# Paged softmax of a decoder layer: the maximum over the partitions moved from GpSimd to TensorE and VectorE

## Chip, cores and metric

One core of a Trainium2 chip runs the whole layer. The metric is the device time of one execution in microseconds (us). The engines are named as the profile does: PE is TensorE's matmul and PEld its weight load, DVE is VectorE, ACT is ScalarE, POOL is GpSimd, SP is SyncE, which here issues DMAs. A trailing q (POOLq, SPq) is an engine's sequencer.

## What is computed

One step of a decoder layer for two kinds of input at once: a prompt of 1024 tokens (plus 16 meta tokens) and eight sequences that each decode one token against 4096 cached keys and values in pages of 128. Every token goes through a projection, differential attention (4 heads, two softmax maps each) beside a causal convolution, an output projection and a SwiGLU FFN. The change touches the decoding sequences' attention alone:

```python
def sample_layer(x, ck, cv, conv_state, page_table, lw, li):
    ...
    k_past = ck[page_table].reshape(Bd, past, N_DIFF_HEADS, 2, HEAD_DIM).astype(k.dtype)
    v_past = cv[page_table].reshape(Bd, past, N_DIFF_HEADS, V_HEAD_DIM).astype(v.dtype)
    ...
    o = diff_attend(q, k_all, v_all, q_pos, k_pos, lam, alibi_slopes())

def diff_attend(q, k, v, q_pos, k_pos, lam, slopes):
    s = jnp.einsum('bqhjd,bkhjd->bhjqk', q, k) * (HEAD_DIM ** -0.5)
    s = s - slopes[None, :, None, None, None] * dist
    ...
    p = jax.nn.softmax(s, axis=-1)
    a = p[:, :, 0] - lam * p[:, :, 1]
    return jnp.einsum('bhqk,bkhe->bqhe', a.astype(v.dtype), v)
```

## The kernel before

The prompt is worked in stages that overlap: projections and convolution, attention by head `h` and block `i` of 128 queries (`attn`), output projection by blocks (`c_one`), then the FFN in steps of 128 hidden columns (`ffn`). Its f32 matmuls are three fp32r matmuls of a high and a low part (`mm3`, L149 to L151); ACT casts the high part of each weight tile and DVE or POOL subtracts to get the low one (L138 and L140 before the FFN, L957 and L959 in it).

The paged attention of the eight sequences is cut into units that are sprinkled over the prompt's work. A unit of keys (`dec_scores`) loads two pages of 128 keys through SP's queue, multiplies each with the query by one POOL instruction (L681), and one DVE instruction sums the products to scores (L691); keys lie on the partitions, so `s` is 128 partitions by 33 pages by 8 maps (the 33rd page is the token itself). Sixteen units are one sequence. Then `dec_max` adds the bias (L699), puts in the token's own score (L704), takes the maximum over the pages on DVE (L706, giving 128x8), and takes it over the partitions with POOL's `partition_all_reduce` (L708). `dec_exp` subtracts it on DVE (L713) and takes the exponential on ACT (L714). A unit of values (`dec_values`) loads two pages of values; in groups of two units PE multiplies them with the probabilities as weights (L733), four pages side by side in four column groups of the array.

`dec_units` sets the order of units: 23 units of keys first (16 and a lag of 7); then, as soon as the tokens' own keys exist (`"k" in nat`), maximum and exponential of the first sequence at once, and after that two units of values and two of keys in turn. A later sequence's exponential is written two units of keys (`elag`) after its maximum. `dec_step` takes units at given rates: about one a block of attention, one a block of `c_one`, 2.45 at each `fill` of the FFN. When the units are used up, the eight tokens' own output projection and FFN (`sample_units`) follow in the same way. All is emitted with a priority 400 instructions ahead, and the framework's planner, which simulates a timeline, sets the final order on each engine; every engine then works its instructions in that order. SP's queue carries page loads, weight loads and most others, in order; a load whose buffer is not free holds up those behind it.

Other names used later: in `attn`, POOL's power L565 (`or`) normalises four blocks of a head, ACT's L567 applies it, PE's L572 transposes the result; DVE's L510 evaluates a score tile that PE's L508 and L509 wrote. `natural` (L607) transposes 128x8 tiles to 8x128 on PE, `row_T` (L1102) transposes 8x128 pieces. PSUM tiles from `pb` come from a ring of three.

Of the kernel before, what the change touches and what calls it, by code (L numbers as in the profile page):

```python
# [12 lines left out]
ALU = mybir.AluOpType  # L13
AX = mybir.AxisListType
SP = mybir.EngineType.SP

P = 128
# [3 lines left out]
DB = 8  # L21
# [25 lines left out]
def tile_layer(ctx: ExitStack, tc: tile.TileContext, I, O, cfg):  # L47
    nc = tc.nc
    V, S, G, T, D = nc.vector, nc.scalar, nc.gpsimd, nc.tensor, nc.sync
# [5 lines left out]
    at = ctx.enter_context(tc.tile_pool(name="at", bufs=cfg["at"]))  # L55
# [33 lines left out]
    def pdec(name):  # L89
        return ps.tile([P, 512], F32, tag="d", name=name, bufs=cfg["nd"])  # L90

    def smt(name, w, n=2, dt=F32):
        return sm.tile([P, w], dt, tag="".join(x for x in name if not x.isdigit()), name=name, bufs=n)
# [5 lines left out]
    ident = cst.tile([P, P], F32, name="ident")  # L99
# [387 lines left out]
    def attn(h, i):  # L487
# [95 lines left out]
    nat = {}  # L583
# [6 lines left out]
    ones = cst.tile([P, DB], F32, name="ones")  # L590
# [4 lines left out]
        out=own, in_=own, pattern=[[-1, DB], [0, 8]], compare_op=ALU.is_equal, fill=0.0, base=0, channel_multiplier=1  # L595
# [60 lines left out]
    def page_pair(src, b, pg, name):  # L656
        t = kv(name)[:, :1024].rearrange("p (i n) -> p i n", i=2)
        for i in range(2):
            n = b * NPG + pg + i
            lds, (v,) = nc.values_load_multi_w_load_instructions(  # L660
                pts[0:1, n : n + 1], engines=[SP], min_val=0, max_val=n_pool - 1
            )
            if len(page_dmas) >= 8:
                for ld in lds:
                    tc.add_manual_dep(ld.ins if hasattr(ld, "ins") else ld, page_dmas[-8], behind, reason="few registers at once")
            x = D.dma_start(t[:, i, :], src[bass.DynSlice(v, 1)].rearrange("o p f -> (o p) f"))  # L666
            if cfg["anchor"] and i == 0:
                tc.add_manual_dep(x.ins if hasattr(x, "ins") else x, point["now"], behind, reason="paced by the prompt's work")
            page_dmas.append(x.ins.name if hasattr(x, "ins") else x.name)
        return t  # L670

    def dec_scores(b, st):
        qB = dec.tile([P, 512], F32, tag="qB", name=f"qB{b}")
        D.dma_start(qB, qsD[b].partition_broadcast(P))
        s = dec.tile([P, NPG + 1, 8], F32, tag="s", name=f"s{b}", bufs=3)
        st[b] = s
        for pg in range(0, NPG, 2):
            kt = page_pair(ck, b, pg, f"k{b}_{pg}")
            n = b * NPG // 2 + pg // 2
            for i in range(2):  # L680
                x = G.tensor_tensor(kt[:, i, :], kt[:, i, :], qB, op=ALU.mult)  # L681
            products.append((s[:, pg : pg + 2, :], kt))
            if len(products) > cfg["rlag"]:
                head_sums(x)
            yield b

    products = []

    def head_sums(after):
        s, kt = products.pop(0)  # L690
        x = V.tensor_reduce(  # L691
            s.rearrange("p a c -> p (a c)"), kt.rearrange("p a (c d) -> p (a c) d", d=HD), axis=AX.X, op=ALU.add
        )
        if after is not None:
            tc.add_manual_dep(x.ins, after.ins.name, behind, reason="sums behind a later product")

    def dec_max(b, st):
        s = st[b]
        V.tensor_tensor(  # L699
            s[:, :NPG, :].rearrange("p g (h j) -> p (g h) j", j=2),  # L700
            s[:, :NPG, :].rearrange("p g (h j) -> p (g h) j", j=2),
            dbias.rearrange("p g h -> p (g h)").unsqueeze(2).to_broadcast([P, NPG * NH, 2]), op=ALU.add,
        )
        V.tensor_copy(s[:, NPG, :], selfs[:, b, :])  # L704
        m = smt(f"dm{b}", 8, 2)
        V.tensor_reduce(m, s.rearrange("p g c -> p c g"), axis=AX.X, op=ALU.max)  # L706
        mg = smt(f"dg{b}", 8, 2)
        G.partition_all_reduce(mg, m, P, bass.bass_isa.ReduceOp.max)  # L708
        st[b] = s, mg

    def dec_exp(b, st):
        s, mg = st[b]
        V.tensor_tensor(s, s, mg.unsqueeze(1).to_broadcast([P, NPG + 1, 8]), op=ALU.subtract)  # L713
        S.activation(s, s, AF.Exp)  # L714
        st[b] = s

    def dec_total(b, s):
        V.tensor_reduce(dsum[:, b, :], s.rearrange("p g c -> p c g"), axis=AX.X, op=ALU.add)
        V.tensor_tensor(selfa, selfa, s[:DB, NPG, :], op=ALU.add)

    def dec_values(b, st):
        a = st.pop(b)
        pv = pdec(f"pv{b}")
        vs = []
        for pg in range(0, NPG, 2):
            if not vs:
                size = min(cfg["vgrp"] if kv_n[1] else 2, (NPG - pg) // 2)
            vs.append((pg, page_pair(cv, b, pg, f"v{b}_{pg}")))
            if len(vs) == size:
                for q, vt in vs:  # L730
                    for i in range(2):
                        g = (q + i) % 4
                        x = T.matmul(  # L733
                            pv[32 * g : 32 * g + 8, :], lhsT=a[:, q + i, :], rhs=vt[:, i, :],
                            start=q + i < 4, stop=q + i >= NPG - 4, tile_position=(0, 32 * g),
                        )
                        if vt is not vs[-1][1]:
                            tc.add_manual_dep(x.ins, page_dmas[-1], together, reason="pages side by side")
                vs = []
            if pg == NPG // 2:  # L740
                dec_total(b, a)
            yield 0 if vs else size
        pvs = dec.tile([P, 512], F32, tag="gs", name=f"pvs{b}", bufs=2)
        for g in range(4):
            S.copy(pvs[32 * g : 32 * g + 8, :], pv[32 * g : 32 * g + 8, :])
            S.dma_start(pvD[b, g], pvs[32 * g : 32 * g + 8, :])

    def dec_units():
        st = {}
        ks = (b for bb in range(DB) for b in dec_scores(bb, st))  # L750
        nk, ready, exped, at = 0, 0, 0, []
        per = NPG // 2

        def softmaxes(all_=False):
            nonlocal ready, exped
            while "k" in nat and ready < (nk - len(products)) // per:
                dec_max(ready, st)
                at.append(nk)
                ready += 1
            while exped < ready and (all_ or nk >= at[exped] + cfg["elag"]):  # L760
                dec_exp(exped, st)
                exped += 1

        def keys(n):
            nonlocal nk
            for _ in range(n):
                if nk < DB * per:
                    next(ks)
                    nk += 1
                    if nk == DB * per:  # L770
                        while products:
                            head_sums(None)
                    softmaxes(nk == DB * per)
                    yield

        yield from keys(per + cfg["lag"])
        while "k" not in nat:
            yield "wait"
        softmaxes(True)
        for b in range(DB):  # L780
            for n in dec_values(b, st):
                yield
                yield from keys(n)

    dgen = dec_units()
    dst = {"done": False}

# [601 lines left out]
    sqv=1, ksp=0, asp=1, sps=1,  # L1389
    od=1, kt=0, ho=0,  # L1390
    wd='d',
    lag=7, rlag=1, elag=2,
    xn_g=(), wi_first=1, wi_e=(13, 17), sq=0,
    behind=-400, w0=7, w1=7, wi_n=1, anchor=1, wi_v=(8, 9, 10, 11, 12), taps=11, conv=400, r2_g=1, hb=5,
    vgrp=2, fing=5, ml_g=0, fend=22, cst=0, db=3, cn=6, scn=12, wo0=27, wor=2, c0=7,
    at=8, slabs=35, kv=4, p=6, dve_mul=0, rate_b=(1, 1.25, 1, 0.75), rate_c=1, rate_d=2.45, rate_s=2.2,
# [42 lines left out]
```

## Time and profile before

| | before |
|---|---|
| median of 3 runs | 1437.51 us (1437.06 to 1437.9) |
| the profiled execution | 1439.89 us |
| span of its trace | 1437.8 us |
| mean granted clock of PE | 0.976 of full speed |
| busy: PE, DVE, POOL, ACT | 1350.5, 861.1, 592.1, 548.6 us |
| HBM traffic | 183 GB/s over the span |

The trace is of one execution; its span is what the engines worked, and the execution's time holds a few microseconds around it. Busy times of different engines overlap. Matmuls are pipelined, so the end of one is modelled, and the spacing of starts says more than a duration. An idle time in brackets stands before the instruction, with what was read as its releaser; "issue" means that nothing in the profile was waited for.

### The profile page before, as it was taken

How to read it: one execution, taken by the hardware profiler on the slowest of the kernel's cores; microseconds unless marked ns; L12 is line 12 of the kernel's file. 1: busy time of each engine (PE TensorE's matmuls, PEld its weight loads, DVE VectorE, ACT ScalarE, POOL GpSimd, SP SyncE). 2: the span in 40 equal slices, each digit the busy share in tenths (PEclk: the TensorE clock that was granted, in tenths of full speed). 3: DMA queues.
4: the chain of work that ended last, by engine and by line, in shares of the span. 5: the costliest groups of instructions: out<-in, count | busy, mean ns of one | idle time of the engine just before them, and what ended most of it. 6: DMA issues, size and time to landing. Idle time of an engine off the chain costs nothing.

```text
span 1437.8 us, 21538 instructions
## 1 busy us (share of the span) xinstructions
PE 1350.5 (94%) x6960; PEld 1058.9 (74%) x6960; DVE 861.1 (60%) x1403; ACT 548.6 (38%) x1110; POOL 592.1 (41%) x479
## 2 busy tenths in 40 slices
PE   5999899988848999999999989999999999999997
PEld 4999799978847787777776767777676666567666
DVE  5689995854674567455846546474744176363157
ACT  6566878797855345212222121212121112211122
POOL 4498875544454123544636536464650000000023
PEclk9999899999979999999999999999999999999999
DMA  8210113416335538678776767787677736663554
GB/s 248 84 59 17 44 45 116 135 63 210 111 121 180 182 126 265 233 229 272 251 254 220 241 217 241 243 260 255 229 243 246 254 114 201 239 217 128 176 205 177
DMA packets 199678, 264.35 MB, mean 184 GB/s; under 512 B 16423, under 2 KB 99816, under 8 KB 199557
## 3 DMA queue, kind: packets, MB, share of 16 engines
q1 hardware_dynamic: 188912, 254.40, 53.8%
q10 hardware_dynamic: 10653, 8.57, 1.8%
q8 instruction: 55, 0.90, 0.3%
q14 instruction: 58, 0.48, 0.1%
HBM read 245.92 MB, written 17.48 MB: 183 GB/s over the span
## 4 chain that ended last, share of the span: by engine, by line
PE 48%; SPq 5%; DMA 5%; issue 4%; DVE 4%; POOL 3%; ACT 1%; POOLq 0%; DVEq 0%; ACTq 0%
PE pu L149 4%; PE pu L151 4%; PE pu L150 4%; PE pg L150 4%; PE pg L149 4%; PE dn L149 4%; PE pg L151 4%; PE dn L150 4%; PE dn L151 4%; PE pv L733 3%; DMA k<-in_cache_k 3%; SPq L666 3%; SPq L660 2%; PE mo L151 2%; PE mo L149 2%
## 5 line engine op out<-in xcount | busy, mean ns | idle before, releaser
L681 POOL TENSOR_TENSOR k<-k,qB 128x512 f32<-128x512 f32 x256 | 353.3, 1407 | 230.5 <-DMA k<-in_cache_k 159.7
L691 DVE TENSOR_REDUCE s<-k 128x16 f32<-128x1024 f32 x128 | 155.2, 1213 | 99.1 <-POOL k L681 99.0
L957 ACT CAST wH<-wr 128x1024 fp32r<-128x1024 f32 x66 | 69.1, 1048 | 239.2 <-DVE wL L959 137.3
L149 PE MATMUL dn<-wH,aH 128*128 128x512 f32 x352 | 141.9, 406 | 4.0 <-DVE y L1000 2.3
L150 PE MATMUL dn<-wL,aH 128*128 128x512 f32 x352 | 141.4, 402 | 0.0
L151 PE MATMUL dn<-wH,aL 128*128 128x512 f32 x352 | 141.3, 402 | 0.0
L149 PE MATMUL pu<-hH,wH 128*128 128x512 f32 x352 | 140.1, 398 | 0.5 <-DVE y L1000 0.5
L151 PE MATMUL pu<-hH,wL 128*128 128x512 f32 x352 | 138.7, 395 | 1.5 <-DVE wL L959 1.5
L149 PE MATMUL pg<-hH,wH 128*128 128x512 f32 x352 | 139.8, 397 | 0.0
L150 PE MATMUL pu<-hL,wH 128*128 128x512 f32 x352 | 139.5, 396 | 0.0
L150 PE MATMUL pg<-hL,wH 128*128 128x512 f32 x352 | 139.4, 396 | 0.0
L151 PE MATMUL pg<-hH,wL 128*128 128x512 f32 x352 | 139.1, 395 | 0.0
L959 DVE TENSOR_TENSOR wL<-wr,wH 128x1024 fp32r<-128x1024 f32 x66 | 92.4, 1399 | 46.6 <-ACT wH L957 19.8
L1000 DVE TENSOR_TENSOR y<-dn,y 128x512 f32<-128x512 f32 x144 | 95.8, 684 | 38.8 <-PE dn L151 38.2
L415 POOL TENSOR_TENSOR cb<-cb 128x512 f32<-128x512 f32 x80 | 103.0, 1319 | 18.3 <-ACT cb L412 9.8
L424 DVE SCALAR_TENSOR_TENSOR acc<-u,cw,acc 128x512 f32<-128x512 f32 x144 | 98.5, 747 | 0.2
L1072 POOL TENSOR_TENSOR y<-y,wfpost 128x512 f32<-128x512 f32 x10 | 14.2, 1424 | 202.0 <-ACT ft L1070 202.0
L149 PEld LDWEIGHTS dn<-wH,aH 128*128 128x128 f32 x352 | 67.8, 193 | 29.2 <-issue 6.9
L983 ACT CAST aH<-sg 128x512 fp32r<-128x512 f32 x44 | 27.2, 619 | 161.8 <-DVE sg L976 161.7
L150 PEld LDWEIGHTS dn<-wL,aH 128*128 128x128 f32 x352 | 67.4, 192 | 25.9 <-issue 10.0
L149 PEld LDWEIGHTS pu<-hH,wH 128*128 128x128 f32 x352 | 66.1, 188 | 25.9 <-issue 9.9
L149 PEld LDWEIGHTS pg<-hH,wH 128*128 128x128 f32 x352 | 66.1, 188 | 24.3 <-issue 8.6
(581 smaller groups left out, 2923.5 us busy)
## 6 DMA issues: line engine op xcount, KB each, us to landing
k<-in_cache_k SPq DMA_DIRECT2D x256, 256.0 KB
v<-in_cache_v SPq DMA_DIRECT2D x256, 256.0 KB
wr<-in_w_gate SPq DMA_DIRECT2D x22, 512.0 KB
wr<-in_w_up SPq DMA_DIRECT2D x22, 512.0 KB
wr<-in_w_down SPq DMA_DIRECT2D x22, 512.0 KB
sd<-in_w_down SPq DMA_DIRECT2D x22, 512.0 KB
sw_gate<-in_w_gate SPq DMA_DIRECT2D x20, 512.0 KB
sw_up<-in_w_up SPq DMA_DIRECT2D x20, 512.0 KB
```

What stands on the lines that cost most here:

```text
L149: T.matmul(out, lhsT=wH, rhs=xH, start=first, stop=False)
L150: T.matmul(out, lhsT=wH, rhs=xL, start=False, stop=False)
L151: mark(T.matmul(out, lhsT=wL, rhs=xH, start=False, stop=last))
L415: G.tensor_tensor(accp, accp, t, op=ALU.add)
L424: V.scalar_tensor_tensor(dst, src, cw[:, ct, k : k + 1], acc, op0=ALU.mult, op1=ALU.add)
L666: x = D.dma_start(t[:, i, :], src[bass.DynSlice(v, 1)].rearrange("o p f -> (o p) f"))
L681: x = G.tensor_tensor(kt[:, i, :], kt[:, i, :], qB, op=ALU.mult)
L691: x = V.tensor_reduce(s.rearrange("p a c -> p (a c)"), kt.rearrange("p a (c d) -> p (a c) d", d=HD), axis=AX.X, op=ALU.add)
L733: x = T.matmul(pv[32 * g : 32 * g + 8, :], lhsT=a[:, q + i, :], rhs=vt[:, i, :], start=q + i < 4, stop=q + i >= NPG - 4, tile_position=(0, ...
L957: S.copy(H[:, :1024], raw[:, :1024])
L959: V.tensor_tensor(L[:, :1024], raw[:, :1024], H[:, :1024].bitcast(F32), op=ALU.subtract)
L1000: V.tensor_tensor(y[b][:, ws], o, y[b][:, ws], op=ALU.add)
```

## The change

The maximum over the partitions becomes four small steps. `dec_rows` transposes the 128x8 maxima on PE to 8x128 in PSUM, reduces each row on DVE to 8x1, and multiplies the 8x8 identity with it on DVE, which gives a diagonal of the eight maxima. `dec_spread` multiplies a matrix of ones (8x128) with that diagonal on PE, so that all 128 partitions get the eight maxima, and copies them out of PSUM on DVE. `dec_exp` is as before. These three are written as steps in `dec_units`: `advance` is called at every unit, of keys or of values, starts at most one maximum, and moves each softmax that is under way by one step when `sgap` = 2 units have passed. Before the values of a sequence start, units of keys are written until its exponential is there, or, if keys may not run further ahead, empty units; this puts the first sequence's values some seven units of keys later.

```diff
--- before.py
+++ after.py
@@ -704,8 +704,24 @@
         V.tensor_copy(s[:, NPG, :], selfs[:, b, :])
         m = smt(f"dm{b}", 8, 2)
         V.tensor_reduce(m, s.rearrange("p g c -> p c g"), axis=AX.X, op=ALU.max)
+        st[b] = s, m
+
+    def dec_rows(b, st):
+        s, m = st[b]
+        pt = pb(f"mT{b}")
+        T.transpose(out=pt[:8, :P], in_=m, identity=ident)
+        g = smt(f"mr{b}", 1, 2)
+        V.tensor_reduce(g[:8], pt[:8, :P], axis=AX.X, op=ALU.max)
+        d = smt(f"md{b}", 8, 2)
+        V.tensor_scalar(d[:8], ident[:8, :8], g[:8], None, op0=ALU.mult)
+        st[b] = s, d
+
+    def dec_spread(b, st):
+        s, d = st[b]
+        pt = pb(f"mB{b}")
+        T.matmul(pt[:, :8], lhsT=ones[:8, 0:1].to_broadcast([8, P]), rhs=d[:8], start=True, stop=True)
         mg = smt(f"dg{b}", 8, 2)
-        G.partition_all_reduce(mg, m, P, bass.bass_isa.ReduceOp.max)
+        V.tensor_copy(mg, pt[:, :8])
         st[b] = s, mg
 
     def dec_exp(b, st):
@@ -748,18 +764,24 @@
     def dec_units():
         st = {}
         ks = (b for bb in range(DB) for b in dec_scores(bb, st))
-        nk, ready, exped, at = 0, 0, 0, []
+        nk, ready, exped, units, under = 0, 0, 0, 0, []
         per = NPG // 2
-
-        def softmaxes(all_=False):
-            nonlocal ready, exped
-            while "k" in nat and ready < (nk - len(products)) // per:
+        steps = (dec_rows, dec_spread, dec_exp)
+
+        def advance():
+            nonlocal ready, exped, units
+            units += 1
+            for x in list(under):
+                if units >= x[2] + cfg["sgap"]:
+                    steps[x[1]](x[0], st)
+                    x[1:] = x[1] + 1, units
+                    if x[1] == len(steps):
+                        under.remove(x)
+                        exped += 1
+            if "k" in nat and ready < (nk - len(products)) // per:
                 dec_max(ready, st)
-                at.append(nk)
+                under.append([ready, 0, units])
                 ready += 1
-            while exped < ready and (all_ or nk >= at[exped] + cfg["elag"]):
-                dec_exp(exped, st)
-                exped += 1
 
         def keys(n):
             nonlocal nk
@@ -770,15 +792,21 @@
                     if nk == DB * per:
                         while products:
                             head_sums(None)
-                    softmaxes(nk == DB * per)
+                    advance()
                     yield
 
         yield from keys(per + cfg["lag"])
         while "k" not in nat:
             yield "wait"
-        softmaxes(True)
         for b in range(DB):
+            while exped <= b:
+                if nk < min(DB * per, per * (b + 2) - 1):
+                    yield from keys(1)
+                else:
+                    advance()
+                    yield
             for n in dec_values(b, st):
+                advance()
                 yield
                 yield from keys(n)
 
@@ -1389,7 +1417,7 @@
     sqv=1, ksp=0, asp=1, sps=1,
     od=1, kt=0, ho=0,
     wd='d',
-    lag=7, rlag=1, elag=2,
+    lag=7, rlag=1, sgap=2,
     xn_g=(), wi_first=1, wi_e=(13, 17), sq=0,
     behind=-400, w0=7, w1=7, wi_n=1, anchor=1, wi_v=(8, 9, 10, 11, 12), taps=11, conv=400, r2_g=1, hb=5,
     vgrp=2, fing=5, ml_g=0, fend=22, cst=0, db=3, cn=6, scn=12, wo0=27, wor=2, c0=7,
```

## Rows read from the trace of the kernel before

**Rows 1.** The page, part 1: busy time of each engine, share of the span, instructions.

```profile
PE 1350.5 (94%) x6960; PEld 1058.9 (74%) x6960; DVE 861.1 (60%) x1403; ACT 548.6 (38%) x1110; POOL 592.1 (41%) x479
```

**Rows 2.** Five stages: width, busy PE, PEld, DVE, ACT, POOL, PEclk, DMA, GB/s.

```profile
427.00:437.00 10.00, 9.27 (x45) 8.74 (x45) 6.72 (x21) 8.90 (x19) 5.84 (x4) 0.55 0.07 28
...
456.00:740.00 284.00, 283.18 (x1321) 212.69 (x1320) 171.27 (x233) 85.77 (x171) 121.80 (x99) 1.00 0.69 225
740.00:775.00 35.00, 31.94 (x137) 22.40 (x137) 16.72 (x19) 9.99 (x14) 16.92 (x13) 0.90 0.62 203
...
828.00:862.00 34.00, 29.57 (x131) 20.72 (x130) 16.23 (x19) 8.34 (x12) 13.13 (x10) 0.95 0.63 217
...
1090.00:1145.00 55.00, 55.00 (x268) 35.46 (x267) 13.34 (x19) 6.97 (x12) 0.00 (x0) 1.00 0.73 241
```

**Rows 3.** Instructions of L708 and L140: count, ns min/median/max, first and last start.

```profile
L708 POOLq MODIFY_POOL_CONFIG  x16: 8/11/25, 401.6 to 1076.3; - x16
...
L140 POOLq MODIFY_POOL_CONFIG  x2: 108/108/108, 410.1 to 410.1; - x2
```

**Rows 4.** Groups by line: busy, mean ns, idle time before and its releasers.

```profile
L708 POOL PARTITION_ALL_REDUCE dg<-dm x8 | 3.1, 393 | 57.9 <-issue 35.9 <-DMA k<-in_cache_k 22.0
...
L713 DVE TENSOR_TENSOR s<-s,dg 128x264 f32<-128x264 f32 x8 | 3.5, 434 | 46.3 <-POOL dg L708 46.3
```

**Rows 5.** POOL's timeline: start, us, instruction, [idle before <-releaser].

```profile
409.71 0.39 POOL L708 PARTITION_ALL_REDUCE dg<-dm  x1 [8.11 <-issue]
417.32 2.33 POOL L140 TENSOR_TENSOR wo2L<-wo2r,wo2H 128x1024 fp32r<-128x1024 f32 x1 [7.21 <-DMA wo7r<-in_w_out]
...
424.87 1.37 POOL L565 TENSOR_TENSOR or<-ssq,mhalf 128x4 f32<-128x4 f32 x1
...
672.99 17.97 POOL L681 TENSOR_TENSOR k<-k,qB 128x512 f32<-128x512 f32 x12 [8.59 <-DMA k<-in_cache_k]
...
744.84 0.39 POOL L708 PARTITION_ALL_REDUCE dg<-dm  x1 [5.93 <-issue]
752.96 11.52 POOL L681 TENSOR_TENSOR k<-k,qB 128x512 f32<-128x512 f32 x8 [7.72 <-PE pu L151]
```

**Rows 6.** PE's timeline, five of its waits between 400 and 1145 us.

```profile
412.23 0.69 PE L508 MATMUL S<-R,L 128*128 128x392 f32 x1 [5.41 <-DVE nm L510]
...
426.73 0.47 PE L572 MATMUL oT<-ident,oh 128*128 128x128 f32 x1 [9.24 <-ACT oh L567]
...
768.19 1.90 PE L733 MATMUL pv<-v,s 128*8 128x512 f32 x8 [3.06 <-DMA v<-in_cache_v]
...
855.57 1.63 PE L733 MATMUL pv<-v,s 128*8 128x512 f32 x8 [3.95 <-DMA v<-in_cache_v]
...
1017.31 0.50 PE L149 MATMUL dn<-wH,aH 128*128 128x512 f32 x1 [1.68 <-DVE y L1000]
```

**Rows 7.** ACT's cast of wo2, from the timeline.

```profile
401.99 1.04 ACT L138 CAST wo2H<-wo2r 128x1024 fp32r<-128x1024 f32 x1
```

**Rows 8.** The chain of waits, 740 to 775 us: start, us, what.

```profile
752.96 2.54 POOL k L681 x2
755.53 1.23 DVE s L691
...
763.38 4.67 DMA v<-in_cache_v
```

**Rows 9.** The chain of waits, 826 to 862 us.

```profile
834.77 7.08 issue
```

**Rows 10.** Small PE operations in the timeline and the chain, and a weight load's gap.

```profile
386.73 0.60 PE L607 MATMUL nk<-ident,smp 128*8 128x128 f32 x4 [0.57 <-ACT kst L308]
...
1206.37 0.59 PE shT L1102 x8
...
569.24 0.19 PEld L150 LDWEIGHTS pg<-hL,wH 128*128 128x128 f32 x1 [0.86 <-issue]
```

**Rows 11.** Who waited for whom: us in total, times, the longest.

```profile
POOL k L681 <- DMA k<-in_cache_k: 159.7, 48, 9.5
```

## Prediction

> **What bounds the kernel now.** I read the page first, then one-line tables by stage, then the POOL queue, then every wait of TensorE (PE). The page says that PE is busy 1350.5 of 1437.8 us [rows 1], so only about 87 us can be won without taking work off PE, and any wait of another engine that PE doesn't feel is worth nothing. By stage, PE is full in the prompt's FFN: 283.18 us busy of 284 from 456 to 740, and 55.00 of 55 from 1090 to 1145, where pages of values still arrive but no keys are multiplied any more [rows 2]. The holes lie before 456 us (end of the prompt's attention) and in two places near 768 and 855 us, and each comes with a stretch in which the granted clock fell: mean 0.55 from 427 to 437, 0.90 from 740 to 775, 0.95 from 828 to 862 [rows 2]. The two levels are 1.2 and 2.4 GHz, so a mean of 0.90 is a fifth of the stretch at 1.2 GHz, and a stretch of width w with mean c has lost w x (1 - c) of full-speed PE time wherever PE was busy.
>
> Next the line that is changed. Ahead of each of the eight all-reduces stand two MODIFY_POOL_CONFIG, and two stand again at the next ordinary POOL instruction (for the first softmax at L140, at 410.1 us) [rows 3]. The all-reduce itself is 0.393 us, but POOL idles 57.9 us before the eight, 7.2 each, and VectorE (DVE) waits 46.3 us for them [rows 4]. The POOL queue shows the other half: 8.11 us before the all-reduce at 409.71 and 7.21 us before the next instruction, 5.93 and then 7.72 us at 744.84, and 8.59 us, the longest, behind the one at 664 [rows 5]. The releasers named for the gaps behind vary (a DMA, PE); their length hardly does, so I read them as one thing, the change of configuration back. So one softmax takes about 15 us out of POOL for 0.4 us of work, and about 6 us out of DVE, whose next instruction is the subtraction that waits.
>
> **What of this reaches PE.** Listing PE's waits shows where it counts: 5.41 us at 412.23 (DVE behind the first all-reduce), 9.24 us at 426.73, 3.06 us at 768.19, 3.95 us at 855.57, 1.68 us at 1017.31 [rows 6]. In the other softmaxes (580, 664, 921, 1083 us) PE runs on through DVE's stall, because its weights are split ahead.
>
> **Part by part.**
>
> *A, the first softmax (removed).* The wait at 426.73 is for ACT's L567, which needs POOL's `or` at 424.87, which stands in POOL's queue behind wo2L at 417.32 [rows 5]. POOL's hole in front of wo2L is 8.11 + 0.39 + 7.21 = 15.7 us. Without it wo2L would start when its cast is done: POOL was free at about 401.6, the cast ends at 401.99 + 1.04 = 403.03 [rows 7], so 417.32 - 403.1 = 14.2 us earlier, and `or` and PE's L572 with it. The 5.41 us at 412.23 lie inside these 14.2 and are not added. Against it: the new order puts up to seven units of keys in front of the first values (below), and a unit costs POOL two products; one more unit in front of `or` is 2 x 1.29 = 2.6 us by the chain's 2.54 [rows 8]. I take 14.2 - 2.6 = 11.6. The ends: 14.2 + 10 x (1 - 0.55) = 18.7, if the clock stays at 2.4 GHz in 427 to 437, which I don't count since ACT is busy 8.90 us of those 10 [rows 2]; and 6, with three such units.
>
> *B, the stalls at 768 and 855 (removed).* The chain of waits in 740 to 775 runs POOL products at 752.96 (right after the reload), DVE's sums at 755.53, the page loads that SP had held back for the buffers of those sums, value pages on their way from 763.38 for 4.67 us, PE [rows 8]. The chain to the wait at 855.57 begins with 7.08 us of "issue" on POOL at 834.77, just behind an all-reduce, and then runs the same way [rows 9]. Worth 3.06 + 35 x (1 - 0.90) + 3.95 + 34 x (1 - 0.95) = 3.06 + 3.5 + 3.95 + 1.7 = 12.2 us. Ends: 0, if value pages are late anyway; 13.9 with the 1.68 us at 1017.31, 15 us after an all-reduce.
>
> *C, work added on PE.* Per softmax a transpose of 128x8 and a spread of 8 rows to 128 partitions, which I count as two instructions since an f32 matmul of pages (L733) is two in this trace (512 for 256 pages). Nearest rows: four transposes of the same form in 0.60 us, eight 8x8 ones in 0.59 us [rows 10], so 0.15 + 2 x 0.074 = 0.30 us. Leaving the FFN's stream costs something too; behind a group of page matmuls the weight load shows a gap of 0.86 us, part of which the group itself covers [rows 10]. Ends: 8 x 0.30 = 2.4 and 8 x (0.30 + 0.86) = 9.3. I take 0.5 each, 4 us, nearer to the rows of the operations.
>
> *D, waits added on PE.* The transpose waits for DVE's L706, the spread for DVE's product with the identity; behind either stands the FFN's stream, for which everybody waits. Both come two units after what they need, and the exponential two more. PE waits on DVE in the FFN are rare, the longest before 1145 us is 1.68 [rows 6]. Ends: 0 and 16 x 1.68 = 27 us. I take 0.25 each, 4 us, because at the stage where 14 of the 16 lie PE runs without one for hundreds of microseconds [rows 2].
>
> *E, order.* Values of the first sequence start some seven units later, all else keeps its place, and the number of units is the same. One group of page matmuls that filled PE's idle time before 456 us now runs in the full stream: 1 us (0 to 1.2). The end then has some seven more units of values alone, and such a stretch runs with PE full [rows 2]: nothing. DVE gets three small instructions a softmax; by the 0.434 us of the subtraction as their upper bound [rows 4] 24 x 0.434 = 10.4 us against 46.3 us of waiting removed, on an engine busy 60% [rows 1]: nothing. Two more PSUM tiles from the ring of three are held for one DVE instruction each: nothing in the FFN, where that ring is idle; in the attention it would show as one more wait of the sort in D.
>
> Sum: -11.6 - 12.2 + 4 + 4 + 1 = -14.8 us. The profiled execution took 1439.89 us, its span is 1437.8, the median of the runs 1437.51; the difference comes from the span and is taken off the median: 1422.7 us. After A and B, what is late next is PE itself.
>
> *A rule that speaks against it.* The rows above say that a 0.393 us reduction costs POOL about 15 us. The Trainium skill, GPSIMD Engine Reference, section 4.1 (Engine selection), names GPSIMD as the engine for a reduction along the partitions and VectorE as the one not to use. By the instruction's own row that would be right; by the holes around it the trace disagrees. By that rule the sum would lose A and B and keep C, D and E.
>
> **The rivals.**
> - *More comes back* (0.12): both upper ends, 18.7 + 13.9, with C at 2.4 and no new waits: 1437.5 - 30.2 = 1407.3. For it: the clock's share is real time; against: ACT is nearly full behind A.
> - *Value pages are late anyway* (0.12): A stays, B is 0: 1437.5 - 11.6 + 9 = 1434.9. POOL waits 159.7 us for key pages in 48 places [rows 11], which no all-reduce explains; but the holes in PE come just behind the reloads.
> - *PE waits for DVE* (0.11, slower): in the added steps PE, which now is independent of the softmax, is held by DVE, which in turn sits behind sums whose products are late. At 1.68 us a step: -11.6 - 12.2 + 4 + 27 + 1 = +8.2, 1445.7, and more if the clock falls to 1.2 GHz behind it. It decides from (14.8 + 4)/16 = 1.2 us a step. For it: DVE's sums follow POOL's products, and those wait up to 9.5 us for pages [rows 11]. Against: two units lie between, and the longest DVE stalls were the ones behind the reloads.
> - *The reloads stay* (0.03, slower): another POOL instruction needs the other configuration, so the change keeps the holes and adds C, D and E: 1437.5 + 9 = 1446.5. Against: the pairs stand at L708 and at what follows it, nowhere else.
>
> **How the numbers follow.** The forecast, 1422.7, gets 0.62; its own range is 1410 to 1432. The range for 8 in 10 reaches down past the first rival and up past the second: 1405 to 1441; it leaves out the two slower rivals (0.14) and a tail. About 0.2%, 2.9 us, is what a measurement can tell from no change, so faster means under 1434.6. Faster: 0.59 of the forecast, 0.12, and 0.05 of the second rival, 0.76. Same: 0.03 + 0.06 = 0.09. Slower: 0.11 + 0.03 + 0.01 = 0.15.
>
> **What would show it.** Right: no MODIFY_POOL_CONFIG and no POOL gap of 7 us at "issue" in the paged stretch; no DVE wait of 5 to 7 us at the subtraction; PE's wait for L567 at 2 us or less and the FFN starting some 12 us earlier; no PE wait of 3 us for value pages and a clock of 1.00 through 460 to 1145. C and D are read from PE's rows of mT and mB and the waits in front of them. Wrong: waits of PE in front of mT or mB of over 1 us on average; PE holes for value pages as large as before; or the order around 400 us so changed that the attention's end is no earlier.

## The result, and the profile after

The changed kernel takes 1422.62 us in the median of four runs (1419.89 to 1423.39), beside 1437.55 (1437.06 to 1437.9) for the kernel before: a ratio of 0.9898, interval 0.9885 to 0.9912. The profiled execution took 1423.16 us; its span is 1421.5, against 1437.8.

The page of the kernel after: its span; its busy times, as in [rows 1]; and the shares of the chain that ended last.

```profile
span 1421.5 us, 21564 instructions
...
PE 1350.6 (95%) x6984; PEld 1058.3 (74%) x6984; DVE 873.5 (61%) x1427; ACT 549.4 (39%) x1110; POOL 589.5 (41%) x471
...
PE 78%; DVE 10%; ACT 6%; DMA 3%; issue 2%; POOL 1%; DVEq 0%; POOLq 0%; ACTq 0%; SPq 0%
```

PE has the 24 instructions more that were counted and the same busy time as before. What went is idle time: 16.3 us of it. Of the 34 MODIFY_POOL_CONFIG of the trace before, the 32 around the eight all-reduces are gone; the two that are left stand at 1.6 us, at the making of the identity, as before (the prediction had them nowhere but at the softmaxes). POOL has the eight all-reduces fewer (479 to 471).

The stages of [rows 2] in the kernel after, with the end of the attention in front of them and five microseconds of the FFN between (columns as there).

```profile
399.00:412.00 13.00, 9.30 (x60) 7.82 (x58) 13.00 (x32) 10.81 (x32) 11.45 (x8) 1.00 0.50 189
412.00:427.00 15.00, 9.23 (x32) 6.71 (x32) 13.37 (x33) 9.02 (x18) 9.80 (x6) 0.57 0.05 19
427.00:437.00 10.00, 7.24 (x53) 6.38 (x52) 9.89 (x19) 6.74 (x22) 7.05 (x6) 0.97 0.47 138
456.00:740.00 284.00, 282.09 (x1309) 210.34 (x1308) 177.15 (x243) 84.54 (x157) 118.19 (x96) 0.99 0.68 222
563.00:568.00 5.00, 5.00 (x15) 3.85 (x15) 3.73 (x7) 1.66 (x2) 3.28 (x3) 0.66 1.03 365
740.00:775.00 35.00, 35.00 (x165) 24.80 (x164) 19.02 (x21) 4.66 (x7) 22.59 (x16) 1.00 0.78 259
828.00:862.00 34.00, 34.00 (x158) 24.84 (x157) 19.77 (x25) 6.90 (x9) 16.53 (x13) 1.00 0.78 260
```

740 to 775 and 828 to 862 are now full at 1.00; in [rows 2] they were 31.94 of 35 and 29.57 of 34, at 0.90 and 0.95. The attention's end is not full. PE is busy 9.23 of 15 us from 412 to 427, at a mean clock of 0.57. Before, the clock was low from 412 to 427 too (0.62) and stayed low from 427 to 437 ([rows 2]); that second stretch is now at 0.97. The third engine column shows what is full instead: DVE is busy 13.00 of 13 us and then 13.37 of 15.

Where the 16.3 us came from is read off the same instructions in both traces. The first `mo` matmul (the output projection's first) starts at 444.5 us instead of 452.2, so 7.7 us were gained by the end of the attention, of which 1.5 are there already at the transposes `nk` (385.2 us, before 386.7 in [rows 10]), ahead of everything that was changed: scatter between two executions. The last `pv` starts 15.6 us earlier (1127.5, 1143.1), the last `dn` 16.4 (1412.6, 1429.0). So about 6.2 us belong to the attention, 7.9 to the FFN with its two former holes (15.6 - 7.7), and 0.8 to the end. This scatter has to be kept in mind with every start below: in the traces of nine of the fourteen kernels, which run the same instructions in the same order on every engine up to `nk`, `nk` starts anywhere from 382.0 to 386.7 us. From `nk` to the first `mo` it is 65.5 us before and 59.3 after.

### The profile page after: what moved, and what is told of

Same layout as the page of the kernel before. It is cut to its first block, busy times and chain, and to the rows that moved or that the text cites. A ratio compares the mean times of both kernels' runs of the same rounds, so it can differ in the third digit from the quotient of the medians.

```text
span 1421.5 us, 21564 instructions
## 1 busy us (share of the span) xinstructions
PE 1350.6 (95%) x6984; PEld 1058.3 (74%) x6984; DVE 873.5 (61%) x1427; ACT 549.4 (39%) x1110; POOL 589.5 (41%) x471
## 4 chain that ended last, share of the span: by engine, by line
PE 78%; DVE 10%; ACT 6%; DMA 3%; issue 2%; POOL 1%; DVEq 0%; POOLq 0%; ACTq 0%; SPq 0%
PE pg L149 7%; PE pg L150 7%; PE pg L151 7%; PE pu L149 6%; PE pu L151 6%; PE pu L150 6%; PE dn L149 5%; PE dn L151 5%; PE dn L150 5%; PE pv L749 4%; PE mo L149 2%; PE mo L150 2%; PE mo L151 2%; DVE p L527 2%; PE o L549 2%
## 5 line engine op out<-in xcount | busy, mean ns | idle before, releaser
L681 POOL TENSOR_TENSOR k<-k,qB 128x512 f32<-128x512 f32 x256 | 354.4, 1411 | 263.7 <-DMA k<-in_cache_k 213.5
L691 DVE TENSOR_REDUCE s<-k 128x16 f32<-128x1024 f32 x128 | 154.9, 1212 | 64.2 <-POOL k L681 64.1
L987 DVE TENSOR_TENSOR wL<-wr,wH 128x1024 fp32r<-128x1024 f32 x66 | 91.2, 1381 | 72.4 <-ACT wH L985 23.7
L1004 DVE TENSOR_TENSOR sg<-sg,pu 128x512 f32<-128x512 f32 x44 | 30.1, 684 | 93.2 <-PE pu L151 74.7
L151 PEld LDWEIGHTS pu<-hH,wL 128*128 128x128 f32 x352 | 66.3, 188 | 24.1 <-issue 6.0
```

What stands on the lines that cost most here:

```text
L151: mark(T.matmul(out, lhsT=wL, rhs=xH, start=False, stop=last))
L691: x = V.tensor_reduce(s.rearrange("p a c -> p (a c)"), kt.rearrange("p a (c d) -> p (a c) d", d=HD), axis=AX.X, op=ALU.add)
L987: V.tensor_tensor(L[:, :1024], raw[:, :1024], H[:, :1024].bitcast(F32), op=ALU.subtract)
L1004: V.tensor_tensor(sg, sg, o, op=ALU.mult)
```

## The attention's end: POOL was freed and DVE was next

POOL's timeline of the kernel after at the place of [rows 5].

```profile
401.64 2.40 POOL L140 TENSOR_TENSOR wo2L<-wo2r,wo2H 128x1024 fp32r<-128x1024 f32 x1 [1.55 <-issue]
404.00 4.11 POOL L681 TENSOR_TENSOR k<-k,qB 128x512 f32<-128x512 f32 x3
408.04 2.42 POOL L140 TENSOR_TENSOR wo3L<-wo3r,wo3H 128x1024 fp32r<-128x1024 f32 x1
410.39 1.63 POOL L681 TENSOR_TENSOR k<-k,qB 128x512 f32<-128x512 f32 x1
411.98 1.05 POOL L565 TENSOR_TENSOR or<-ssq,mhalf 128x4 f32<-128x4 f32 x1
```

`or` starts at 411.98 instead of 424.87: 12.9 us earlier, or 11.4 without the 1.5 of scatter, close to the 11.6 of the prediction. But ACT, which applies it, comes at 419.72 only, and PE waits for others. Here are three of PE's waits in the kernel after: the longest of the attention's end, the one for L567, and the longest in the FFN's stream.

```profile
414.67 0.66 PE L508 MATMUL S<-R,L 128*128 128x352 f32 x1 [4.94 <-DVE nm L510]
...
437.88 0.33 PE L572 MATMUL oT<-ident,oh 128*128 128x128 f32 x1 [1.68 <-ACT oh L567]
...
563.00 0.47 PE L149 MATMUL pu<-hH,wH 128*128 128x512 f32 x1 [1.91 <-DVE mr L714]
```

The wait of 9.24 us for L567 in [rows 6] is gone; the largest wait is one for L510, DVE's evaluation of a score tile. DVE is late because it is full, and part of that is that its instructions take longer beside POOL at work. First a row of the kernel before, in POOL's hole in front of its all-reduce; then three rows of DVE and one of POOL in the kernel after; last the group of the softmaxes' subtraction after (busy us, mean ns, idle us). A row with x2 can hold two shapes: the one at 408.59 is a 128x400 and a 128x128.

```profile
404.22 0.63 DVE L527 SCALAR_TENSOR_TENSOR p<-p,cc,p 128x400 f32<-128x400 f32 x1
```

```profile
402.70 1.76 DVE L527 SCALAR_TENSOR_TENSOR p<-p,cc,p 128x400 f32<-128x400 f32 x1
408.59 3.57 DVE L527 SCALAR_TENSOR_TENSOR p<-p,cc,p 128x400 f32<-128x400 f32 x2
...
418.04 1.17 DVE L527 SCALAR_TENSOR_TENSOR p<-p,cc,p 128x400 f32<-128x400 f32 x2
...
418.84 2.60 POOL L140 TENSOR_TENSOR wo5L<-wo5r,wo5H 128x1024 fp32r<-128x1024 f32 x1 [3.48 <-ACT wo5H L138]
...
L729 DVE TENSOR_TENSOR s<-s,dg 128x264 f32<-128x264 f32 x8 | 8.6, 1072 | 0.2
```

L527 adds two softmax maps, both in SBUF. The same 128x400 takes 0.63 us where POOL stands still and 1.76 where POOL works on wo2L (401.64 to 404.04). The subtraction, also of two SBUF operands, went from 434 ns in [rows 4] to 1072: POOL's stall had given DVE a quiet neighbour. So part of what POOL's hole cost came back as DVE's time.

It is the smaller part. The kernel before has such long L527 too, later, when POOL works again behind its hole. From the same instruction of DVE up to the first `mo`, all engines and then L527 alone (DVE busy); the first two rows are the kernel before, the others the kernel after:

```profile
399.00:452.20 53.20, 31.91 (x198) 28.08 (x198) 34.08 (x86) 32.37 (x87) 27.80 (x18) 0.81 0.41 134
399.00:452.20 53.20, 12.92 (x12) 0.81 0.41 134
...
397.50:444.50 47.00, 32.67 (x201) 27.57 (x201) 41.56 (x91) 32.64 (x88) 34.23 (x23) 0.85 0.43 151
397.50:444.50 47.00, 14.09 (x12) 0.85 0.43 151
```

DVE has 7.5 us more to do in a stretch that is 6.2 us shorter. L527 is 1.2 of that. Two more sums of key products (L691, six instead of four) are 2.3, the subtraction of the output projection's inputs (L930) 2.0, the first softmax's subtraction 1.8 (2.20 instead of 0.43) and the new small steps 0.7.

## Experiments: which part of the change is it?

**The new order with the old all-reduce.** Rival: the gain comes from the order of the units, and the engine matters little.

```diff
     def dec_rows(b, st):
         s, m = st[b]
-        (transposition, row maximum, diagonal)
+        mg = smt(f"dg{b}", 8, 2)
+        G.partition_all_reduce(mg, m, P, bass.bass_isa.ReduceOp.max)
+        st[b] = s, mg
     def dec_spread(b, st):
+        pass
```

> The new order of units with the old all-reduce on POOL in place of the transposition, so the exponential comes four units after it and DVE need not stand and wait. Theory (POOL's holes of 7 us before and behind each all-reduce are what cost): the holes are back, key pages' buffers come free late again, PE waits for value pages of 3 to 4 us return: 1432 to 1440. Rival (it was the order that helped, DVE no longer waiting 46 us): 1416 to 1421, below the changed kernel, since the added PE work is gone too.

1451.74 us, ratio 1.0086 (1.0044 to 1.0127): the order alone makes the kernel slower, by more than was expected. Two stages and the longest of PE's waits in the FFN:

```profile
456.00:740.00 284.00, 276.93 (x1271) 206.76 (x1270) 164.64 (x227) 84.14 (x168) 107.31 (x93) 0.99 0.66 212
740.00:1090.00 350.00, 339.05 (x1540) 243.32 (x1539) 197.27 (x219) 72.05 (x95) 175.93 (x132) 0.98 0.73 242
...
932.43 1.90 PE L740 MATMUL pv<-v,s 128*8 128x512 f32 x8 [4.66 <-DMA v<-in_cache_v]
```

The same eight holes now also cost PE 7 us in the first of these stages, which [rows 2] shows nearly full (283.18). The first `mo` comes 72.2 us behind `nk`, where it was 65.5 before. The order is no source of the gain; it moves the holes to places that happen to be worse.

**The old order with the new engines.** The transposition, maximum, diagonal and spread written at the place of the all-reduce, no steps, no gap.

```diff
     (dec_max of the kernel before)
-        G.partition_all_reduce(mg, m, P, bass.bass_isa.ReduceOp.max)
+        (the lines of dec_rows and dec_spread, one behind the other)
+        V.tensor_copy(mg, pt[:, :8])
```

> The old order of units, with transposition, row maximum, diagonal and spread written straight after the maximum over the pages. Theory (POOL's holes): no holes, so near the changed kernel, 1420 to 1430; what it is above 1422.6 is the price of steps without a gap, PE in front of mT and mB waiting for DVE. Rival (the order helped): 1437.6 plus the added work, 1440 to 1446.

1421.02 us, 0.9883 (0.9855 to 0.991): nothing tells it from the kernel after. So the gain needs the new engines and not the new order, and within these intervals the spacing of the steps by two units, which terms D and E were about, is neither needed nor harmful: PE is full in 456 to 740 and in 740 to 1090, and its only wait in front of such a step is 0.72 us, in the attention.

**The first softmax on POOL, seven on PE.**

```diff
     def dec_rows(b, st):
         s, m = st[b]
+        if b == 0:
+            mg = smt(f"dg{b}", 8, 2)
+            G.partition_all_reduce(mg, m, P, bass.bass_isa.ReduceOp.max)
+            st[b] = s, mg
+            return
     def dec_spread(b, st):
+        if b == 0:
+            return
```

> The changed kernel with the first of the eight softmaxes alone taking its maximum by the all-reduce on POOL. In the trace of the changed kernel the first output projection starts 7.7 us earlier than before, of which 1.5 us are there before the first softmax. Theory (the holes at the first softmax hold up the end of the attention): 1426 to 1431. Rival (the attention's end is now set by DVE, so a hole in POOL there is covered, and all of the gain lies in the later seven): 1420 to 1424.

1430.55 us, 0.9947 (0.9926 to 0.9968). The first hole alone costs 7.9 us over the kernel after; the first `mo` starts at 453.0 instead of 444.5, and 69.5 us behind `nk` instead of 59.3. That is term A by another way: 8 by the time and 10 by the trace, not 11.6. The FFN from 740 to 1090 is full, as after. The all-reduces of the other seven cost 21.2 us more than the steps that replace them in this order (1451.74 - 1430.55).

**Without the maximum over the partitions.** The steps stay in place and do nothing, so that each partition subtracts its own maximum; this leaves out part of the softmax.

```diff
     def dec_rows(b, st):
-        (all)
+        pass
     def dec_spread(b, st):
-        (all)
+        pass
```

> The changed kernel without the maximum over the partitions: each partition subtracts its own maximum, transposition, row maximum, diagonal and spread are left out, the order of units stays. It prices the added work and its waits. Theory from the ledger of starts (1.5 scatter + 6.2 at the attention's end + 15 of waits and clock behind the value pages = 22.7 against a span shorter by 16.3): 6 us are paid for the added steps, so 1415 to 1418. Rival (the added steps cost what their durations say, 8 x 0.3 us): 1419 to 1422.

1416.24 us, 0.9847 (0.9821 to 0.9874): all eight maxima by PE and DVE cost 1422.62 - 1416.24 = 6.4 us together. That is C and D, predicted at 8; the order, E, stays as it was. It is also what is left to be won by any cheaper way to the same maximum.

**A longer gap between the steps.** Theory: the one wait of more than a microsecond in the FFN's stream (563.00 above) comes from steps that follow each other too closely, and more units between them save it and its clock loss.

```diff
-    lag=7, rlag=1, sgap=2,
+    lag=7, rlag=1, sgap=4,
```

> The changed kernel with four units between the steps instead of two. In the changed trace PE waits for a step once in the FFN, 1.91 us at 563, and works 3.4 us at 1.2 GHz behind it, 3.6 us together. Theory (the gap is what keeps the steps from waiting): 1417 to 1420. Rival (the gap does nothing, that wait was for a PSUM tile or a weight tile beside it, and the kernel with steps back to back was no slower): 1421 to 1425.

1423.01 us, 0.9911 (0.9883 to 0.9939): no difference, as if the gap did nothing. The wait at 563 is gone and a shorter one of 0.75 us stands at 554, with the clock at 1.00 behind it; from the first `mo` to the end it is 978 us, against 977. So the wait's price, read from its rows, did not come back as time.

## Experiments: is it DVE beside POOL?

Theory: after the change the attention's end hangs on DVE, which POOL's long instructions lengthen. What takes POOL's work away or cuts it up should then shorten L527 and bring `mo` forward; if the end hangs on something else, nothing of that moves it.

**POOL's instructions in quarters.** The subtraction of the output projection's weights, 2.4 us each, in four pieces of 256 columns.

```diff
-        l_eng.tensor_tensor(L[:, :1024], raw[:, :1024], H[:, :1024].bitcast(F32), op=ALU.subtract)
+        n = 1024 // parts
+        for a in range(0, 1024, n):
+            l_eng.tensor_tensor(L[:, a : a + n], raw[:, a : a + n], H[:, a : a + n].bitcast(F32), op=ALU.subtract)
...
-        wo.append(load_split(I["w_out"][0, k * P : (k + 1) * P, :], f"wo{k}", G, n3=False))
+        wo.append(load_split(I["w_out"][0, k * P : (k + 1) * P, :], f"wo{k}", G, n3=False, parts=4))
```

> The changed kernel with POOL's subtraction of each output-projection weight tile (L140 for wo, 2.4 us) cut into four of 256 columns. In the changed trace DVE's L527, which reads two operands from SBUF, takes 1.7 us beside a working POOL and 0.63 us beside an idle one. Theory (DVE stands until POOL's instruction at hand is over): L527 gets shorter by about 1 us each where it meets these, the attention ends 3 to 6 us earlier, 1416 to 1420. Rival (the two share the port element by element, so only the sum of POOL's work counts): L527 as long as before, and four starts instead of one: 1422 to 1427.

1419.29 us, 0.9886 (0.9855 to 0.9917): the time alone shows no difference to the kernel after. The rows do; DVE's two rows, and POOL's pieces beside the first (x4 in 2.83 us, so 0.71 each):

```profile
403.25 1.12 DVE L529 SCALAR_TENSOR_TENSOR p<-p,cc,p 128x400 f32<-128x400 f32 x1
408.07 2.33 DVE L529 SCALAR_TENSOR_TENSOR p<-p,cc,p 128x400 f32<-128x400 f32 x2
...
401.11 2.83 POOL L142 TENSOR_TENSOR wo2L<-wo2r,wo2H 128x256 fp32r<-128x256 f32 x4
```

1.12 in place of 1.76, and 2.33 for two in place of 3.57. The first `mo` starts at 441.6 instead of 444.5, and 55.1 us behind `nk` instead of 59.3: 4.2 us. Much of that is not L527. Beside the quarters DVE's copies, with one SBUF operand each, are shorter as well: L643 (8x64, L645 here) takes 0.54 us instead of 2.17, and the three of L704 (L706 here) take 1.29 instead of 2.49.

**The same subtraction on DVE itself.**

```diff
-        wo.append(load_split(I["w_out"][0, k * P : (k + 1) * P, :], f"wo{k}", G, n3=False))
+        wo.append(load_split(I["w_out"][0, k * P : (k + 1) * P, :], f"wo{k}", V, n3=False))
```

> The changed kernel with the same eight subtractions on DVE instead of POOL (1.2 us each by L959's two-operand rows). POOL is then free in the last head but for key products. Theory (DVE is what the attention's end now waits for, and POOL slows it): 8 x 1.2 = 9.8 us more on DVE against some 10 instructions of L527 that get 1.1 us shorter: no change within 3 us, 1420 to 1426. Rival (POOL's queue in front of L565 is what holds up the end, as the prediction had it): the queue is emptied, 1412 to 1417.

1417.73 us, 0.9876 (0.984 to 0.9913), between the two expectations, and its interval meets that of the kernel after. `mo` starts at 440.1, but only 1.2 us of the 4.4 lie behind `nk`. The work on DVE and the quiet on POOL nearly cancel: by itself this tells nothing apart.

**No units during the last head's attention.** The rate of units there from 0.75 a block to 0, so that neither POOL's products nor DVE's sums stand in it.

```diff
-    at=8, slabs=35, kv=4, p=6, dve_mul=0, rate_b=(1, 1.25, 1, 0.75), rate_c=1, rate_d=2.45, rate_s=2.2,
+    at=8, slabs=35, kv=4, p=6, dve_mul=0, rate_b=(1, 1.25, 1, 0), rate_c=1, rate_d=2.45, rate_s=2.2,
```

> The changed kernel without units of paged work in the last head of the attention (rate 0 instead of 0.75), so the first softmax and its six units move behind the attention. Theory (key products and the steps of the first softmax lengthen the attention's end through DVE): first output projection 5 to 8 us earlier, and six units later at the end of the pages, about 2.5 fills, covered by the FFN: 1413 to 1419. Rival (the attention's end is set by its own work): no change, 1421 to 1425.

1413.81 us, 0.9845 (0.9814 to 0.9877), clear of the kernel after. `mo` starts at 433.9 us, 10.6 earlier, and the end comes 9 us earlier: the later units cost the FFN little. But 4.8 of the 10.6 are there at `nk` already (380.4), where no unit is missing yet (43 key products on POOL from 150 to 385 us, 42 in the kernel after). The planner made another order for this kernel from early on (DVE's differs from 10 us, PE's from 27), as it did for the longer gap, for the subtraction on DVE and for the next two; from 150 to 250 us its granted clock is 0.97 instead of 0.91. What of the 9 us is due to that order is open; the longer gap has it too and is no faster. From `nk` to `mo` it is 53.5 us instead of 59.3. So the paged work in that stretch cost some 6 us there; whether by DVE's own sums or by POOL beside DVE this run doesn't tell.

**Both: no units there, and the weights' subtraction on DVE.** The edits of the last two together.

> The changed kernel with both edits that helped it: no units of paged work in the last head, and the eight subtractions for the output projection on DVE. With the units gone POOL has little left there, so what remains to be saved by taking the subtractions off it is less than alone (4.9 us). Theory (both act on the same stretch, DVE beside a working POOL): 1409 to 1413. Rival (they act on different waits and add up): 1407 to 1409. If the eight subtractions now are DVE's own bound: 1414 to 1418.

1409.49 us, 0.9812 (0.9759 to 0.9864), the best of all: 28 us (1.9%) under the kernel before and 13 under the one after. DVE's L527 and POOL's only instruction of that stretch before 422 us:

```profile
398.74 0.63 DVE L527 SCALAR_TENSOR_TENSOR p<-p,cc,p 128x400 f32<-128x400 f32 x1
...
406.04 1.18 POOL L565 TENSOR_TENSOR or<-ssq,mhalf 128x4 f32<-128x4 f32 x1 [12.12 <-ACT junk L563]
```

With POOL idle for 12 us, L527 is back at 0.63. It does not bring `mo` forward: from `nk` it is 53.4 us, with the units alone gone 53.5, since the eight subtractions are now DVE's. With the units alone gone, wo2L was still on POOL (396.89 to 399.29), and the instruction beside it took 1.76 again:

```profile
397.95 1.76 DVE L527 SCALAR_TENSOR_TENSOR p<-p,cc,p 128x400 f32<-128x400 f32 x1
```

In five kernels, then, the same instruction went by what POOL did: 0.63 before, 1.76 after, 1.12 with short pieces, 1.76 without units, 0.63 here. That DVE slows beside POOL is shown; that this by itself holds up the attention's end is not, since the one run that changes little else, the quarters, has a time that is not clear of the kernel after. Whether the step from the units alone to both edits is more than scatter the times don't say, since their intervals meet.

**No units there, with quarters on POOL.**

> The changed kernel without units in the last head, and POOL's subtractions cut into four. Theory (DVE stands until POOL's instruction at hand is over, and with the key products gone these are the long ones that are left): 1409 to 1413. Rival (without the products DVE has time enough): 1413 to 1416.

1412.98 us, 0.9827 (0.9782 to 0.9872), at the border of the two expectations: not told apart from the kernel without units. Once the units are gone, the pieces bring nothing that can be measured.

**The old order with both edits.** Is the spacing of the steps worth something once the attention's end is clear?

```diff
     (the kernel of the old order with the new engines, and in it)
-    (weights' subtraction) G        (rate of the last head) 0.75
+    (weights' subtraction) V        (rate of the last head) 0
```

> The old order of units with the steps back to back, without units in the last head and with the subtractions on DVE. The old order was as fast as the new one by itself (1421.0 against 1422.6), so: as the first of this set within 3 us, 1408 to 1414. Rival (steps back to back cost once the attention's end is tight): 1415 to 1420.

1417.54 us, 0.9852 (0.9805 to 0.9899), not under 1414 as the theory wanted, and in the range of its rival, that steps back to back cost something. The intervals of this and of the last but one kernel, with both edits, meet, so the times leave it open whether the new order is worth some microseconds here. The traces rather point away from the steps: of the 7.4 us between the two spans 6.2 are there at `nk` (385.3 and 379.1), ahead of the first step, and this kernel has the planner's order of before up to there.

**The kernel before, without units in the last head.** If a hole had a fixed price, this edit would gain here what it gains after.

> The kernel before, all-reduce on POOL and old order, without units of paged work in the last head. It tells whether the 8.8 us of that edit need the change. Theory (the all-reduce costs wherever it stands: moving the first softmax out of the attention saves what the first hole cost there, 6 to 8 us, and the holes behind the value pages stay): 1426 to 1433. Rival (the edit gains as much as it did for the changed kernel plus the first hole): 1420 to 1424. If the holes behind value pages come at worse places: 1435 to 1450.

1452.41 us, 1.0092 (1.0062 to 1.0122): 15 us slower than before, where the same edit brought 9 with the change in place. One stage, three of PE's waits in it, and DVE's wait ahead of the first of them:

```profile
740.00:1090.00 350.00, 325.31 (x1461) 233.23 (x1461) 182.83 (x211) 67.94 (x88) 172.55 (x129) 0.96 0.69 227
...
776.06 0.79 PE L149 MATMUL dn<-wH,aH 128*128 128x512 f32 x1 [5.81 <-DVE y L1000]
862.52 0.79 PE L149 MATMUL dn<-wH,aH 128*128 128x512 f32 x1 [7.29 <-DVE y L1000]
951.83 0.79 PE L149 MATMUL dn<-wH,aH 128*128 128x512 f32 x1 [7.74 <-DVE y L1000]
...
771.90 1.22 DVE L691 TENSOR_REDUCE s<-k 128x16 f32<-128x1024 f32 x1 [12.15 <-POOL k L681]
```

The units are later, and behind the all-reduce at 757.13 DVE stands 12.15 us at a sum of products that POOL has not yet made; `y`, for which PE's next `dn` waits, stands behind that sum in DVE's queue. The same comes again near 862 and 952. It makes 24.7 us of PE idle and 4% of the clock, where before it was 9.8 us, most of them waits for value pages. The attention's end did gain, from `nk` to `mo` 60.7 us instead of 65.5; the FFN lost more. So a hole has no fixed price: at 580 and 664 us in the kernel before it cost PE nothing, here up to 7.74 us.

## Why the prediction was right, and where its steps were not

The total was right (1422.7 forecast, 1422.62 measured) and the mechanism was the one named, but the terms were up to some microseconds off and made up for one another: that the total fits to 0.1 us is luck.

- *The hole of 15 us on POOL per all-reduce:* right. No change of configuration is left in the paged stretch, nor DVE's 46.3 us in front of the subtraction; DVE now waits 8.4 us for the transposes and 11.4 for the spreads, all told.
- *A, 11.6 us:* too high. POOL's `or` moved by 12.9 (11.4 net of scatter), which the step had right; the step that failed was the one that let PE follow POOL. The prediction took PE as what is late next, and DVE was: full from 399 to 412, and with 41.56 us of work up to the first `mo` where it had 34.08. Term E had put DVE's part at nothing, by its busy share of 60% over the whole span and with the subtraction unchanged at 0.434 us; neither holds at the attention's end. The first `mo` gained 6.2 us net of scatter, by the undoing of the first softmax 7.9 to 10.2. All lie above the lower end of 6, whose reason (more units in front of `or`) was another. PE's wait for L567 did fall below 2 us, as said (1.68), and the FFN did not start 12 us earlier.
- *B, 12.2 us:* too low. From 740 to 1090 PE was busy 340.17 of 350 before and is 350.00 of 350 after: 9.8 us of idle, and with the two clock losses of the prediction's working (3.5 + 1.7) 15.0. The 9.8 are five waits; the prediction had summed two of them (3.06 and 3.95), kept the 1.68 at 1017 for the range, and passed over 0.48 at 832 and 0.65 at 939. No wait for a value page is left, so the rival that they are late anyway has fallen. It keeps one point: POOL does wait longer for key pages, 213.5 us in 55 places against the 159.7 of [rows 11], and PE doesn't feel it.
- *C, 4 us:* 5.0 by the rows. The starts of the matmuls about the last spread, and all transposes and spreads of the kernel after (count, ns min/median/max, first and last start):

```profile
1055.43 0.39 PE L149 MATMUL pg<-hH,wH 128*128 128x512 f32 x1
1055.67 0.39 PE L150 MATMUL pg<-hL,wH 128*128 128x512 f32 x1
1055.98 0.38 PE L722 MATMUL mB<-md,ones 8*128 8x8 f32 x2
1056.30 0.51 PE L151 MATMUL pg<-hH,wL 128*128 128x512 f32 x1
1056.64 0.39 PE L149 MATMUL pg<-hH,wH 128*128 128x512 f32 x1
...
L712 PE MATMUL mT<-ident,dm x8: 270/272/421, 421.4 to 1050.7; 128*8 128x128 f32 x8
L722 PE MATMUL mB<-md,ones x16: 251/271/378, 426.6 to 1056.1; 8*128 8x8 f32 x16
```

  The stream steps by 0.23 to 0.24 us (first two rows). From the second `pg` to the fourth it is 0.97, where two steps are 0.46: the spread costs 0.51. By the same reading the transpose at 558.53 costs 0.12 (0.58 between the matmuls two steps apart around it). Six of the seven spreads in the FFN cost 0.51 or 0.52, and six of the seven transposes 0.11 or 0.12. Eight times 0.63 is 5.0. The two instructions that a spread was counted as are there (x16).
- *D, 4 us:* by the rows the size was right, the form not. It isn't a little at each of 16 steps: in front of `mT` and `mB` themselves PE waits nowhere. It is one event, the wait of 1.91 us at 563.00 in front of a `pu`, and behind it 5 us at a clock of 0.66, another 1.7. Its releaser is given as the row maximum (L714), which stood in DVE's queue behind a weight's subtraction (L987) of 2.30 us; that the step was the cause is not shown, and the longer gap took the wait away without a gain in time. The rest is 0.16. The rival that needs 1.2 us a step has fallen.
- *C and D together* were 8 in the sum; the rows add up to 8.8, leaving the steps out shows 6.4, and the 2.4 between these two stay open. By the rows, B less C and D is 15.0 - 5.0 - 3.8 = 6.2, against the 7.9 gained in the FFN; 0.8 of the difference is PE's idle time from 456 to 740 before (283.18 of 284), and the rest, 0.9, is not accounted for.
- *The rule of the Trainium skill that names GPSIMD for such a reduction* (GPSIMD Engine Reference, section 4.1, as the prediction has it): the sum by it, without A and B, would have been 1446.5. The runs show the opposite: with PE and DVE in the all-reduce's place, in either order, the kernel is 1.0% to 1.2% faster than before, while the all-reduce in the new order is 0.9% slower.

## What to carry to other kernels

Cost an instruction by the hole around it, not by its own row: 0.39 us of all-reduce stood in 15 us of POOL's queue, and what that costs depends on who is behind. And when an engine is taken out of the way, ask of the next one two things: was it idle behind the first, and was it faster because the first stood still? A total that comes out right proves no term; undoing the parts one by one does.

## What the runs showed of the hardware

- A DVE instruction with two operands in SBUF takes longer beside a POOL instruction on SBUF, up to that one's end: 128x400 f32 in 0.63 us with POOL idle, 1.76 beside a POOL subtraction of 128x1024, 1.12 beside pieces of 0.71 us. So does a copy with one: L643, 8x64, 2.17 us beside wo0L on POOL, 0.54 beside its quarters, 0.17 with POOL idle (the kernel with both edits). The Trainium skill, SBUF — State Buffer, section "SBUF: two separate sides", says that DVE and GpSimd share one pair of ports as an exclusive lock, held for the whole of an instruction, and that a DVE operation with two SBUF inputs takes part in it against a GpSimd one that reads SBUF. The rows agree: wo2L ends at 404.04, 1.34 us behind the start of L527 at 402.70, and L527 stood 1.13 us longer than alone, to 0.42 us behind wo2L's end; it is 0.42 again without units, and 0.43 behind the fourth piece in the kernel with quarters. And where DVE came first, POOL waited: the pair at 418.04 took its 1.17 us, and wo5L, which began at 418.84, took 2.60 us where the other seven take 2.34 to 2.42.
- An f32 matmul with 8 rows and 8 columns (two instructions) inside a dense stream of fp32r matmuls costs 0.51 us of the stream, a transpose of 128x8 (one instruction) 0.12, although each of these instructions shows about 0.27 us by itself.
- After a wait of PE of only 1.91 us the granted clock was 0.66 for the 5 us that followed (563 to 568), though PE was busy in all five: the loss behind the wait was about as large as the wait. It is not so behind each short wait: behind 1.68 us at 1017 in the kernel before, and behind 2.57 at 697 and 2.83 at 1029 in the new order with the old all-reduce, the clock stayed at 1.00.
